# Quad 0 of the first MLP product as seven half-size products, with its sums taken between the first products of two quads

## The chip, the cores and the metric

The kernel runs on one core of a Trainium2 chip. The metric is the device time of one execution in microseconds (us). Engines are named as in the profile: PE is TensorE (PEld its weight loads), DVE is VectorE, ACT is ScalarE, POOL is GpSimd and SP is SyncE, which only issues DMAs here. POOL issues the DMAs that add to what stands in their destination.

## The reference, cut to what matters

S is 512 rows, D is 1024, the inner width of the MLP is 4096, all in fp32.

```python
def reference(x, positions, g_mix, w_in, ..., w_out, g_mlp, w_ff1, w_ff2, g_final):
    h = x
    for l in range(DEPTH):                                   # DEPTH = 1
        n = rmsnorm(h, g_mix[l])
        proj = n @ w_in[l]
        (gq, gk, gv, gr, z_gf, z_gb, cq, ckv, kr, z_ma, z_mb) = jnp.split(proj, SPLIT_IDX, axis=-1)
        y_gla = gla_branch(gq, gk, gv, gr, z_gf, z_gb, ...)
        y_mla = mla_branch(cq, ckv, kr, positions, ...)
        merged = jax.nn.sigmoid(z_ma) * y_gla + jax.nn.sigmoid(z_mb) * y_mla
        h = h + merged @ w_out[l]
        m = rmsnorm(h, g_mlp[l])
        h = h + jnp.square(jax.nn.relu(m @ w_ff1[l])) @ w_ff2[l]
    return rmsnorm(h, g_final)
```

The change is in `m @ w_ff1`, and in what stands around it.

## The kernel before

**Products.** A factor is split into a high part, a rounded copy made by ACT, and a low part, the rest, made by DVE (`split`). A product is then three matmuls: high by high, high by low, low by high (`mm3`). The large products go by a scheme of seven half-size products: both factors are cut into 2 x 2 blocks, and sums and differences of blocks are multiplied, so that seven products (m = 1 to 7) do what eight would. The prices are sums on DVE and in accumulating DMAs, and splits of these sums.

**The MLP.** The normalized rows (`ms0` to `ms3`, 128 rows each) are transposed by PE (`Flipped`, here `fm`) and split into `m00`, `m10` (columns of the first 256 rows) and `m01`, `m11` (those of the last 256). A *quad* is four blocks of 128 of the 4096 features, a 2 x 2 block product with w_ff1: seven products of 24 matmuls of 128x128 by 128x256. There are eight quads. A *group* is a 2 x 2 block product with w_ff2 over two quads' squared features, into banks `ab` and `mb`. Left operands of the groups are `gh`/`gl`; `four` are split sums of the normalized rows; `hl0h`/`hl0l` to `hl3h`/`hl3l` are a ring of four split weight tiles. The four tiles `ms0` to `ms3` later serve as homes of weight blocks and sums (`wide`, `al_`, `ae_`).

**Quad 0 before.** Its four blocks of features (`f00` to `f03`) are computed plainly, each as 48 matmuls of 256 columns: `hidden_run` for the first half of the rows while the last two row tiles are still being normalized, the rest later (`Plain`, `second_halves`, `pair_plain`). The sums of m for the other quads are made by DVE in `summing` after all of m is transposed and split; they are first used by quad 1's product 5.

**Order.** Everything from the attention on is recorded, and a list scheduler (`Due.order`) lays it down: for each engine it takes what is ready, the one with the earliest latest start first, by its own costs (`Work.cost`), and prints each engine's queue in that order. All recorded instructions have line 232 in the profile. Each engine works through its queue in order. Plain loads stand on SP's queue, accumulating loads (`load_add`) on POOL's.

**Elsewhere.** In the attention, queries `q00`, `q01` and so on are gathered by DMAs on SP's queue, one from `ro0` and one from `ro1` (the two halves of the rotated part) each; `kbuf1` to `kbuf3` get a copy of the rotated key in the same way. `s` is the bank of the scores, `top` its row maximum, `uq` the bank of the projected queries.

Of the kernel before, what the change touches and what calls it, by code (L numbers as in the profile page):

```python
# [11 lines left out]
F32 = mybir.dt.float32  # L12
# [129 lines left out]
class Work:  # L142
# [250 lines left out]
def tile_block(ctx: ExitStack, tc: tile.TileContext, t, out: bass.AP):  # L393
# [143 lines left out]
    class Flipped:  # L537
        def __init__(self, gains, name):
            self.gains, self.name = gains, name
            self.out = {  # L540
                (j, c): [u4(f"{name}{j}{c}{x}", F32R, (P, KD // 2, 256)) for x in range(2)]
                for j in range(2) for c in range(2)
            }
            self.banks = {}
# [10 lines left out]

        def evacuate(self, half, ks=range(KD)):
            for k in ks:
                hi, lo = self.out[k // 4, half]
                src = self.banks[half][k % 4][:, (k // 4) * 256 : (k // 4) * 256 + 256]
                split_scaled(hi[:, k % 4, :], lo[:, k % 4, :], src, self.gains[:, k : k + 1])  # L560
# [1148 lines left out]
    ms_rows = {}  # L1709

    def first_half_square(i, c):
        hparts[i] = sm(f"hp{i}", 4)
        ms_rows[i] = u4(f"ms{i}", F32, (P, D))
        square_half(hrow[i], c, hparts[i], ms_rows[i], True)
# [12 lines left out]

    def hidden_run(begun, half, ks=range(KD)):
        wh, wl, acc = begun
        c = slice(half * HT, (half + 1) * HT)  # L1730
        for k in ks:
            hi, lo = fm.out[k // 4, half]
            mm3(acc[:, c], wh[:, k, :], wl[:, k, :], hi[:, k % 4, :], lo[:, k % 4, :], k == 0, k == KD - 1)
        return acc

    def begin_hidden(j):

        early.append(proj_begin(w1, j * P, f"f0{j}"))
# [91 lines left out]
    w1_sums = [u4(f"w1s{x}", F32, (P, D)) for x in range(2)]  # L1830
    fm = Flipped(gvec[:, V_MLP : V_MLP + 8], "m")
    wo_right[7] = [split_part(B12, 0, "bo7")]
    for rb in range(2):
        add_rows(rb, 1, xs_[rb], ALU.subtract)
    wo_right[7].append(split_part(B12, 1, "bo7"))
    for rb in range(2):
        wo_product(3, (rb,))
        add_rows(rb, 1, zs_[rb])
        second_half_square(rb, 1)
        scaled(rb, row_rstd(hparts[rb]))  # L1840
    wo_right[4] = [split_part(B21, 0, "bo4")]
    wo_product(7, (0,))
    add_rows(2, 1, xs_[0], ALU.subtract)
    wo_right[4].append(split_part(B21, 1, "bo4"))
    flipped(0)
    early = [proj_begin(w1, 0, "f00", "mm")]
    first_half_square(2, 1)
    wo_product(7, (1,), range(2))
    flipped(1)
    wo_product(7, (1,), range(2, NP))  # L1850
    add_rows(3, 1, xs_[1], ALU.subtract)
    fm.evacuate(0)
    first_half_square(3, 1)
    begun_f, lows = begin_late(P, "f01", "mm", w1)
    early.append(begun_f)
    for x in w1_sums:
        nc.sync.dma_start(x.rearrange("p (k w) -> p k w", w=HT), w1_block(1, 1, 0))
    wo_product(4, (0,))
    add_rows(2, 0, xs_[0])
    second_half_square(2, 0)  # L1860
    wo_product(4, (1,))
    add_rows(3, 0, xs_[1])
    rs2 = row_rstd(hparts[2])
    second_half_square(3, 0)
    lows()
    rs3 = row_rstd(hparts[3])
    scaled(2, rs2)
    scaled(3, rs3)
    hidden_run(early[0], 0)
    hidden_run(early[1], 0, range(5))  # L1870
    flipped(2)
    flipped(3)
    for x, other in zip(w1_sums, ((1, 1), (0, 0))):
        nc.gpsimd.dma_start(x.rearrange("p (k w) -> p k w", w=HT), w1_block(1, *other), accum_op=ALU.add)
    for j in (2, 3):
        begin_hidden(j)
    fm.evacuate(1)
    hidden_run(early[1], 0, range(5, KD))
# [36 lines left out]
    rows_ = Ring("row", [u2(f"row{n}") for n in range(4)])  # L1915
    sums_ = Ring("sum", [(u2(f"sy{n}"), u2(f"sz{n}")) for n in range(2)])
    parts_ = [[(u2(f"gh{p}{x}", F32R), u2(f"gl{p}{x}", F32R)) for x in range(2)] for p in range(NP)]
    fours = [u4(f"four{n}", F32R, (P, KD // 2, HT)) for n in range(12)] + fm.out[0, 1]
# [33 lines left out]
    def summing():  # L1952
        homes = {(0, 0): (al_[0], ("al", 0)), (1, 1): (al_[1], ("al", 1)),
                 (0, 1): (wide[2], ("ae", 0)), (1, 0): (wide[3], ("ae", 1))}
        r = {}
        for c in range(2):
            for j in range(2):
                hi, lo = fm.out[j, c]
                x, key = homes[j, c]
                x = flat(x, KD // 2)  # L1960
                r[j, c] = x, key
                dve(FULL, (lambda x=x, hi=hi, lo=lo: nc.vector.tensor_tensor(x, raw(hi), raw(lo), op=ALU.add)),
                    m_key_of(j, c), (key,))

        def combine(o, a, b, op):
            dve(FULL, lambda: nc.vector.tensor_tensor(r[o][0], r[a][0], r[b][0], op=op),
                (r[a][1], r[b][1]), (r[o][1],))

        A, B, C, Dd = (0, 0), (1, 1), (0, 1), (1, 0)
        combine(A, A, C, ALU.subtract)  # L1970
        combine(C, B, C, ALU.subtract)
        combine(B, B, A, ALU.add)
        combine(Dd, B, Dd, ALU.subtract)
        return {5: r[A], 6: r[B], 7: r[C], 4: r[Dd]}

    def m_key_of(j, c):
        n = 2 * j + c
        return (("m", 2 * n), ("m", 2 * n + 1))

    def split_m(m, src, n):  # L1980
        x, key = src
        hi, lo = m_tiles[2 * n], m_tiles[2 * n + 1]
        k = (("ms", 2 * n), ("ms", 2 * n + 1))
        keys = (key,)
        if m == 6:
            act(FULL, lambda: nc.scalar.activation(hi, x, AF.Copy, scale=-1.0), keys, k[:1])
            dve(FULL, lambda: nc.vector.scalar_tensor_tensor(
                lo, x, -1.0, raw(hi), op0=ALU.mult, op1=ALU.subtract), keys + k[:1], k[1:])
        else:
            act(FULL, lambda: nc.scalar.activation(hi, x, AF.Copy), keys, k[:1])  # L1990
            dve(FULL, lambda: nc.vector.tensor_tensor(lo, x, raw(hi), op=ALU.subtract), keys + k[:1], k[1:])
        m_of[m], m_key[m] = (hi, lo), k

    m_of[1], m_of[2], m_of[3] = fm.out[0, 0], fm.out[1, 0], fm.out[1, 1]
    m_key[1], m_key[2], m_key[3] = m_key_of(0, 0), m_key_of(1, 0), m_key_of(1, 1)
# [56 lines left out]
    class Plain:  # L2052


        def __init__(self, j):
            self.j, self.key = j, ("f", j)

        def multiply(self):
            j = self.j
            used = sum((m_key_of(a, b) for a in range(2) for b in range(2)), (("hl", j, 0), ("hl", j, 1)))  # L2060

            def run():
                for half in range(2):
                    hidden_run(early[j], half)

            plan.add("PE", 5.5, run, used, (self.key,))

        def evacuate(self, dst, key):
            act(HALFT, lambda: nc.scalar.activation(dst, early[self.j][2], AF.Relu), (self.key,), (key,))

    class Quad:


        def __init__(self, q):
            self.q, self.banks, self.row = q, {}, {}
# [4 lines left out]
        def fetch(self):  # L2080
            (a, e), (ka, ke) = ae_[self.q % 2], ae_key[self.q % 2]
            self.a, self.e, self.ka, self.ke = flat(a, KD // 2), flat(e, KD // 2), ka, ke
            if self.q == 1:
# [6 lines left out]
        def weights(self, m):  # L2090
            k = KD // 2
            if m in (1, 2, 4):
                item, x, key = staged(self.rows(*{1: (0, 0), 2: (0, 1), 4: (1, 1)}[m]), k)
                ready = prepare(x, key, k)
                if m == 2:
                    self.c = item, x, key
                else:
                    wfs.back(item)
# [41 lines left out]
        def evacuate(self, m, bkey, acc):  # L2140
# [13 lines left out]
            if m == 2:  # L2154
                lefts[p].first(x, key)
            elif m == 3:
                self.pair(p, "px", "qx")
# [200 lines left out]
    plains = [Plain(j) for j in range(4)]  # L2358

    def pair_plain(p):  # L2360
        (kp, px), (kq, qx) = rows_.take(), rows_.take()
        item = sums_.take()
        ykey, (y, z) = item
        for x, (dst, key) in enumerate(((y, ykey), (z, ykey + ("z",)))):
            plains[2 * p + x].evacuate(dst, key)
            c = slice(x * HT, (x + 1) * HT)
            act(QUART, (lambda dst=dst, c=c: nc.scalar.activation(px[:, c], dst[:, 0:HT], AF.Square)), (key,), (kp,))
            act(QUART, (lambda dst=dst, c=c: nc.scalar.activation(qx[:, c], dst[:, HT:S], AF.Square)), (key,), (kq,))
        sums_.free.insert(0, item)
        lefts[p].first(px, kp)  # L2370
        lefts[p].summed(px, qx, kp, kq)
        rows_.back((kp, px))
        rows_.back((kq, qx))

    def second_halves():
        for k in range(KD):
            for e in early[:2]:
                hidden_run(e, 1, (k,))

# [84 lines left out]
```

## Time and profile before

| | |
|---|---|
| Median of 3 runs | 742.14 us (741.44 to 743.15) |
| The profiled execution | 742.11 us, of which the span of the trace is 740.4 us |
| PE | 730.2 us busy (99%), 4238 matmuls and transposes |
| DVE | 606.2 us (82%) |
| ACT | 512.2 us (69%) |
| POOL | 193.6 us (26%) |
| Granted TensorE clock | 1.00 in all stages shown |

A busy share is an average over stages. PE counts as busy while a matmul is in its pipeline. Of the span, the stretch from 404 to 480 us holds the end of the output projection, the transposes of the normalized rows, quad 0, quad 1 and the first group; from 480 us on, groups and quads alternate at an even pace.

### The profile page before, as it was taken

Reading aid. Unit: us, or ns where it says so; the run is one execution under the profiler, and the core shown is the slowest. Engines: PE = TensorE matmul, PEld = TensorE weight load, DVE = VectorE, ACT = ScalarE, POOL = GpSimd, SP = SyncE. Lnnn points to the kernel's source line nnn. Section 1 sums busy time; section 2 is a strip of 40 time slices with the busy share of each in tenths; the row PEclk is TensorE's granted clock in tenths of the full one; section 3 lists DMA queues with packets and bytes.
Section 4 is the critical chain, followed back from the end, with each engine's and each line's share of the span. In section 5 each row is a group of like instructions: output and inputs, shape, how many; then the busy total and the mean of one; then the engine's idle time right before and its main releaser. Section 6 shows DMA issues by size and latency. Waiting matters only on the chain.

```text
span 740.4 us, 11575 instructions
## 1 busy us (share of the span) xinstructions
PE 730.2 (99%) x4238; PEld 643.3 (87%) x4238; DVE 606.2 (82%) x956; ACT 512.2 (69%) x855; POOL 193.6 (26%) x203
## 2 busy tenths in 40 slices
PE   9999999999999999999999999999999999999996
PEld 7888888888888888899988999889988998889985
DVE  7695776759999679998988899868896798778885
ACT  7574665669999566989856788546864587448754
POOL 1133040301211115038753102321122202312433
PEclk9999999999999999999999999999999999999998
DMA  9969895752313214239976449999899997988993
GB/s 312 327 142 168 224 192 107 118 112 57 98 46 68 39 38 109 56 99 246 270 207 98 115 119 222 208 228 201 207 203 212 212 206 178 220 220 191 194 167 115
DMA packets 103930, 121.24 MB, mean 164 GB/s; under 512 B 16080, under 2 KB 67296, under 8 KB 103872
## 3 DMA queue, kind: packets, MB, share of 16 engines
q0 software_dynamic: 30384, 48.52, 38.9%
q1 hardware_dynamic: 73200, 71.45, 31.7%
q8 instruction: 33, 0.54, 0.3%
q10 hardware_dynamic: 288, 0.52, 0.2%
q14 instruction: 25, 0.20, 0.1%
HBM read 116.81 MB, written 2.10 MB: 161 GB/s over the span
## 4 chain that ended last, share of the span: by engine, by line
PE 87%; DVE 5%; DMA 3%; ACT 2%; issue 1%; POOL 1%; POOLq 0%; DVEq 0%; ACTq 0%
PE mb L232 21%; PE ab L232 14%; PE zb L232 4%; PE f L232 3%; PE av L232 3%; PE wox L232 3%; PE gvx L232 3%; PE zax L232 3%; PE grx L232 3%; PE first L232 3%; PE s L232 2%; DMA ms<-in_w_ff 2%; PE cq L232 2%; PE tp L232 2%; PE gvz L232 1%; PE ckv L232 1%
## 5 line engine op out<-in xcount | busy, mean ns | idle before, releaser
L232 POOL DMA_DIRECT2D ms<-in_w_ff x37 | 46.7, 1370 | 115.7 <-DVE hl0l L232 34.7
L232 POOL DMA_DIRECT2D w1s<-in_w_ff x18 | 23.0, 1276 | 90.7 <-DVE hl0l L232 26.9
L232 DVE TENSOR_TENSOR h<-h,ab 128x512 f32<-128x512 f32 x48 | 31.7, 682 | 6.4 <-PE ab L232 6.4
L232 ACT ACTIVATE row<-row 128x512 f32<-128x512 f32 x49 | 30.7, 626 | 1.0
L232 PE MATMUL s<-kbuf,q 96*128 96x512 f32 x96 | 28.3, 408 | 1.4 <-DMA q<-ro 1.4
L232 PE MATMUL av<-pT,v 128*128 128x256 f32 x192 | 28.0, 289 | 0.0
L232 PEld LDWEIGHTS av<-pT,v 128*128 128x128 f32 x192 | 24.8, 190 | 0.5
L232 DVE TENSOR_REDUCE top<-s 128x1 f32<-128x512 f32 x32 | 21.7, 686 | 4.2 <-PE s L232 3.9
L232 ACT ACTIVATE e<-s,top 128x512 f32<-128x512 f32 x32 | 22.0, 695 | 3.9 <-DVE top L232 3.7
L232 PE MATMUL mb<-four,hl0h 128*128 128x256 f32 x128 | 23.4, 283 | 0.0
L232 DVE TENSOR_TENSOR hl1l<-ms,hl1h 128x1024 fp32r<-128x1024 f32 x12 | 14.7, 1224 | 9.9 <-ACT hl1h L232 9.8
L232 DVE TENSOR_TENSOR pT<-tp,pT 128x512 fp32r<-128x512 f32 x32 | 21.6, 682 | 1.1 <-PE av L232 0.5
L232 ACT ACTIVATE row<-mb 128x512 f32<-128x512 f32 x28 | 16.4, 584 | 7.0 <-PE mb L232 7.0
L232 ACT ACTIVATE hl3h<-ms 128x1024 fp32r<-128x1024 f32 x13 | 13.8, 1058 | 10.5 <-PE ab L232 4.6
L232 ACT ACTIVATE pT<-tp 128x512 fp32r<-128x512 f32 x32 | 19.3, 602 | 2.4 <-PE tp L232 2.3
L232 PEld LDWEIGHTS mb<-four,hl0h 128*128 128x128 f32 x128 | 20.1, 192 | 0.5 <-ACT hl2h L232 0.2
L232 PE MATMUL mb<-four,hl3h 128*128 128x256 f32 x112 | 20.4, 283 | 0.0
L232 PE MATMUL mb<-m,hl2h 128*128 128x256 f32 x112 | 20.4, 283 | 0.0
L232 PE MATMUL mb<-four,hl2h 128*128 128x256 f32 x112 | 20.4, 283 | 0.0
L232 ACT ACTIVATE hl1h<-ms 128x1024 fp32r<-128x1024 f32 x12 | 12.7, 1057 | 10.7 <-DMA ms<-in_w_ff 3.7
L232 DVE TENSOR_TENSOR hl3l<-ms,hl3h 128x1024 fp32r<-128x1024 f32 x13 | 15.9, 1223 | 4.9 <-ACT hl3h L232 4.7
L232 PE MATMUL tp<-ident,e 128*128 128x128 f32 x128 | 19.3, 273 | 0.1
(1142 smaller groups left out, 2808.4 us busy)
## 6 DMA issues: line engine op xcount, KB each, us to landing
ms<-in_w_ff POOLq DMA_DIRECT2D x37, 512.0 KB, 7.7
w1s<-in_w_ff POOLq DMA_DIRECT2D x18, 512.0 KB, 6.8
ms<-in_w_ff SPq DMA_DIRECT2D x16, 512.0 KB, 5.1
w1s<-in_w_ff SPq DMA_DIRECT2D x15, 512.0 KB, 6.1
w<-in_w_out POOLq DMA_DIRECT2D x10, 512.0 KB, 9.1
wf0f<-in_w_ff SPq DMA_DIRECT2D x10, 512.0 KB, 6.6
wf1f<-in_w_ff SPq DMA_DIRECT2D x10, 512.0 KB, 6.2
wf2f<-in_w_ff SPq DMA_DIRECT2D x10, 512.0 KB, 5.9
```

The lines of the kernel that those rows point to most:

```text
L232: return call(*map(real, work.args), **{k: real(v) for k, v in work.named.items()})
```

## The change

1. The scheduler's cost of a DMA on SP's queue was 0.06; it is now 0.62 where the DMA reads on-chip memory and 0.45 where it reads HBM. This reorders queues wherever such DMAs stand.
2. Quad 0 becomes a `Quad` like the others. It has two sum tiles of its own (`w0_sums`), and quad 1 keeps its two (`w1_sums`). Products 1 and 2 of quads 0 and 1, which take `m00` and `m10` as they are, stand first; the sums of m (`r00`, `r10`, `r01`, `r11`, `msum`) are taken between and after them, from banks that ACT evacuates whole (`whole`); the split sums for product 5 and 6 are made in halves. Then come products 5 and 6 of both quads in turn, and then 7, 7, 3, 4, 3.
3. In quads 0 and 1 the weights of product 6 get their last block by an accumulating DMA on POOL's queue, not by a DVE add of a staged tile.
4. `m01` is no longer split, there are two more `four` tiles, and quad 1's product 7 leaves the first group.

PE's program falls from 4183 matmuls to 4159, and POOL issues five more DMAs, SP one more.

```diff
     def cost(self):
         n = self.n
         if self.is_dma:
-            return 1.27 if self.engine == "gpsimd" else 0.06
+            return 1.27 if self.engine == "gpsimd" else 0.62 if self.ins else 0.45
...
+        def whole(self, half, ks, to):
+            for k in ks:
+                nc.scalar.activation(to[:, k % 4, :], self.bank(half, k), AF.Copy, scale=self.gains[:, k : k + 1])
...
-    hidden_run(early[0], 0)
-    hidden_run(early[1], 0, range(5))
-    flipped(2)
-    flipped(3)
...
+    def joined(to, j, cols=slice(0, KD // 2)):
+        hi, lo = fm.out[j, 0]
+        nc.vector.tensor_tensor(to[:, cols], raw(hi[:, cols]), raw(lo[:, cols]), op=ALU.add)
+
+    def combine(o, a, b, op, cols=slice(0, KD // 2)):
+        nc.vector.tensor_tensor(o[:, cols], a[:, cols], b[:, cols], op=op)
...
+            elif m == 6 and self.q < 2:
+                load_add(a, self.rows(0, 1), self.ka)
             elif m == 6:
                 item, c, key = self.c
                 dve(FULL, lambda: nc.vector.tensor_tensor(a, a, c, op=ALU.add), (self.ka, key), (self.ka,))
...
-    plan.add("PE", 5.5, second_halves, tuple(("hl", j, x) for j in range(2) for x in range(2)), (("f", 0), ("f", 1)))
-    plains[2].multiply()
-    pair_plain(0)
-    sources = summing()
-    for n, m in enumerate((5, 6, 7, 4)):
-        split_m(m, sources[m], n)
-    plains[3].multiply()
-    quads = {q: Quad(q) for q in range(1, 2 * NQ)}
...
+    quads[0].multiply(1)
+    quads[1].ready(1)
+    quads[0].multiply(2)
+    flipped(2)
+    flipped(3)
+    for x, other in zip(w1_sums, ((1, 1), (0, 0))):
+        nc.gpsimd.dma_start(x.rearrange("p (k w) -> p k w", w=HT), w1_block(1, *other), accum_op=ALU.add)
+    quads[1].ready(2)
+    joined(r00, 0)
+    joined(r10, 1)
+    quads[1].multiply(1)
+    fm.whole(1, range(4), r01)
+    for cols in (slice(0, 2), slice(2, 4)):
+        combine(r00, r00, r01, ALU.subtract, cols)
+        split_m(5, r00, 0, cols)
+    for k in (0, 2):
+        cols = slice(k, k + 2)
+        fm.whole(1, range(4 + k, 6 + k), r11)
+        combine(msum, r11, r00, ALU.add, cols)
+        split_m(6, msum, 1, cols)
+    combine(r01, r11, r01, ALU.subtract)
+    combine(r10, msum, r10, ALU.subtract)
+    quads[1].multiply(2)
+    split_m(7, r01, 2)
+    fm.evacuate(1, range(4, KD))
+    split_m(4, r10, 3)
     groups = [Group(qd) for qd in range(NQ)]
-    w = quads[1]
-    w.multiply(5)
-    pair_plain(1)
-    for m in (1, 2, 6, 3):
-        w.multiply(m)
+    for m in (5, 6):
+        for q in range(2):
+            quads[q].multiply(m)
+    for q, m in ((0, 7), (1, 7), (0, 3), (0, 4), (1, 3)):
+        quads[q].multiply(m)
+    del rows_.free[3:]
     for qd, g in enumerate(groups):
         odd = quads[2 * qd + 1]
         g.multiply(1, 0)
-        odd.multiply(7)
+        if qd:
+            odd.multiply(7)
```

**SP's queue in the attention.** These are the DMAs on SP where the queries of the first heads are gathered; first before, then after.

```order
L232 DMA kbuf1_538_2867<-kbuf0_537_2747 32x1024
L232 DMA kbuf2_539_2918<-kbuf0_537_2747 32x1024
L232 DMA kbuf3_540_2920<-kbuf0_537_2747 32x1024
L232 DMA q00_565_2833<-ro0_555_2895 16x1024
L232 DMA q01_566_2843<-ro0_555_2895 16x1024
L232 DMA q10_587_2930<-ro0_555_2895 16x1024
L232 DMA q11_588_2934<-ro0_555_2895 16x1024
L232 DMA q00_565_2833<-ro1_558_2905 16x1024
```

```order
L232 DMA kbuf1_538_2867<-kbuf0_537_2747 32x1024
L232 DMA q00_565_2833<-ro0_555_2895 16x1024
L232 DMA q00_565_2833<-ro1_558_2905 16x1024
L232 DMA q01_566_2843<-ro0_555_2895 16x1024
L232 DMA q01_566_2843<-ro1_558_2905 16x1024
L232 DMA kbuf2_539_2951<-kbuf0_537_2747 32x1024
```

The second half of `q00` moves from the eighth place of these rows to the third, and the other copies of the key go behind the queries.

**DVE's queue in the first group.** Tile `ms1` holds a block of w_ff2 that is split and then gets another block added by a DMA from POOL; the last row of each piece is the low half of that split. The `sy`, `sz` and `row` tiles hold squared features of the groups' left operands. First before, from the split of `ms0` on; then after, the last nine of the 17 rows that stand between the same split of `ms0` and that of `ms1`, and the latter.

```order
L232 TENSOR_TENSOR hl1l_955_4709<-ms0_894_4290,hl1h_954_4683 128x1024
L232 TENSOR_TENSOR w1s0_903_4189<-w1s0_903_4189,wf1f_950_4501 128x1024
L232 TENSOR_TENSOR sz1_975_4785<-row3_971_4754,sy1_974_4716 128x256
L232 TENSOR_TENSOR hl2l_957_4724<-w1s1_904_4296,hl2h_956_4704 128x1024
L232 TENSOR_TENSOR hl0l_953_4678<-w1s0_903_4189,hl0h_952_4654 128x1024
L232 TENSOR_TENSOR row1_969_4722<-mb2_962_4863,row1_969_4722 128x512
L232 TENSOR_TENSOR hl3l_959_4874<-ms1_896_4316,hl3h_958_4850 128x1024
```

```order
L232 TENSOR_TENSOR sz0_941_4932<-row0_934_4522,sy0_940_4925 128x256
L232 TENSOR_TENSOR hl3l_925_4551<-wf2f_917_4333,hl3h_924_4510 128x1024
L232 TENSOR_TENSOR gl00_945_4965<-sy0_940_4925,gh00_944_4945 128x512
L232 TENSOR_TENSOR row5_939_4792<-mb3_929_4593,row5_939_4792 128x512
L232 TENSOR_TENSOR sy1_942_4873<-sy1_942_4873,row0_934_4522 128x256
L232 TENSOR_TENSOR sz1_943_4982<-row0_934_4522,row2_936_4742 128x256
L232 TENSOR_TENSOR hl0l_919_4409<-wf0f_915_3480,hl0h_918_4395 128x1024
L232 TENSOR_TENSOR four9_969_4984<-row0_934_4522,four9_969_4984 128x512
L232 TENSOR_TENSOR sz1_943_4982<-row0_934_4522,sy1_942_4873 128x256
L232 TENSOR_TENSOR hl2l_923_4529<-ms1_869_4291,hl2h_922_4501 128x1024
```

Before, five rows stand between the two splits; after, 17 (ten of 256 columns, four of 512, three of 1024).

**POOL's queue there.** The rows with `in_w_ff` are accumulating loads; those onto `ms0` and `ms1` bring blocks of w_ff2, those onto `ms2` and `ms3` and the `w0s`, `w1s` tiles blocks of w_ff1. First before, then after.

```order
L232 DMA w1s0_903_4189<-in_w_ff1 128x4x256
L232 DMA ms0_894_4290<-in_w_ff2 128x2x512
L232 DMA ms2_930_4386<-in_w_ff1 128x4x256
L232 DMA ms3_932_4459<-in_w_ff1 128x4x256
L232 DMA ms1_896_4316<-in_w_ff2 128x2x512
```

```order
L232 DMA w1s0_907_4205<-in_w_ff1 128x4x256
L232 DMA w0s0_905_4161<-in_w_ff1 128x4x256
L232 DMA w1s0_907_4205<-in_w_ff1 128x4x256
L232 DMA ms3_871_4465<-in_w_ff1 128x4x256
L232 DMA ms2_870_4453<-in_w_ff1 128x4x256
L232 DMA ms0_868_4252<-in_w_ff2 128x2x512
L232 DMA ms1_869_4291<-in_w_ff2 128x2x512
```

The add onto `ms1` stays last of these; the three others onto `ms` tiles stand in another order before it, behind the new adds onto `w0s0` and `w1s0`.

More of the change, by code (lines that the diff above doesn't have):

```diff
@@ L1829, in tile_block @@
     wo_product(6)
-    w1_sums = [u4(f"w1s{x}", F32, (P, D)) for x in range(2)]
+    w0_sums, w1_sums = ([u4(f"w{q}s{x}", F32, (P, D)) for x in range(2)] for q in range(2))
     fm = Flipped(gvec[:, V_MLP : V_MLP + 8], "m")
[L1832 to L1868, printed above, removed]
-    hidden_run(early[0], 0)
-    hidden_run(early[1], 0, range(5))
-    flipped(2)
-    flipped(3)
[L1873 to L1878, printed above, removed]
     class Plan:
@@ L2050, in split, with ready @@
             dve(HALFT, lambda: nc.vector.tensor_tensor(l, src, raw(h), op=ALU.subtract), (key, k[0]), k[1:])
[L2052 to L2069, printed above, removed]
     class Quad:
         def __init__(self, q):
-            self.q, self.banks, self.row = q, {}, {}
+            self.q, self.banks, self.row, self.begun = q, {}, {}, {}
+        def ready(self, m):
+            self.begun[m] = self.weights(m)
         def rows(self, i, j):
@@ L2356, in tile_block @@
     lefts = [Left(p) for p in range(NP)]
[L2358 to L2373, printed above, removed]
```

125 lines of the change are left out of this document (65 added, 60 removed).

## The prediction

> **What bounds the kernel now.** I read the page first, then the busy times by stage, then the chain and the list of waits for PE, and last the rows around each wait.
>
> ```profile
> span 740.4 us, 11575 instructions
> PE 730.2 (99%) x4238; PEld 643.3 (87%) x4238; DVE 606.2 (82%) x956; ACT 512.2 (69%) x855; POOL 193.6 (26%) x203
> PE 87%; DVE 5%; DMA 3%; ACT 2%; issue 1%; POOL 1%; POOLq 0%; DVEq 0%; ACTq 0%
> ...
> core 0: us, PE busy (x) PEld busy (x) DVE busy (x) ACT busy (x) POOL busy (x), PEclk, DMA share, GB/s
> 404.00:422.00 18.00, 18.00 (x123) 16.43 (x122) 13.32 (x25) 12.14 (x25) 4.17 (x5) 1.00 0.55 140
> 422.00:440.00 18.00, 18.00 (x152) 17.95 (x151) 17.97 (x24) 13.83 (x26) 1.31 (x1) 1.00 0.33 77
> 440.00:466.00 26.00, 26.00 (x190) 24.55 (x189) 25.76 (x39) 22.71 (x36) 5.38 (x5) 1.00 0.91 220
> 466.00:471.00 5.00, 5.00 (x24) 4.14 (x23) 1.31 (x4) 1.34 (x3) 0.81 (x1) 1.00 1.11 301
> 471.00:480.00 9.00, 8.65 (x50) 7.29 (x48) 9.00 (x12) 6.42 (x8) 3.75 (x4) 1.00 0.91 147
> 480.00:721.00 241.00, 240.98 (x1524) 219.25 (x1524) 194.91 (x257) 150.93 (x204) 58.26 (x50) 1.00 0.93 204
> ```
>
> PE is busy 730.2 of 740.4 us, and in the stretch that the change rewrites (404 to 480 us) all but 0.35 of 76 us; from 480 to 721 us it misses 0.02. So PE's own instructions set the time, and an edit counts in two ways only: by matmuls that go, or by a wait of PE that goes or comes. The second engine is DVE: in 404 to 480 us it works 13.32 + 17.97 + 25.76 + 1.31 + 9.00 = 67.36 us, which leaves it 8.6. The granted clock is 1.00 in each of these stages, so I let no term scale.
>
> The profiled execution took 742.11 us, 1.7 more than its span and 0.03 below the median of 742.14. So differences in the span carry over to the median as they are. About 0.2%, 1.5 us, is what a measurement of this kernel can tell from no change.
>
> **Part 1: PE's matmuls, -2.9 us.** Quad 0 was four blocks of 48 matmuls, 192; as seven products of 24 it is 168. All are 128x128 by 128x256.
>
> ```profile
> 554.78 2.87 PE mb L232 x24
> ```
>
> This is one product of the steady part, 24 such matmuls back to back in 2.87 us, 120 ns each. 24 fewer are 2.87 us, and all of it lies on the path as long as PE waits for nothing new. The Trainium skill ("TensorE: Matmul & The Clock Gate", section "Back-to-back issue gap") gives N/2.4 + 2.5 ns for a matmul by itself, which for 256 columns makes 109 ns and, by an estimate, 2.6 us here and a time 0.3 us longer than mine; the trace's 120 ns decides.
>
> **Part 2: the scheduler's price of an SP DMA, -1.4 us.** It moves the queries' copies in the attention.
>
> ```profile
> PE s L232 <- DMA q<-ro: 1.4, 1, 1.4
> ...
> 288.43 1.29 DVE L232 TENSOR_TENSOR ro<-roa,ro 128x512 fp32r<-128x512 f32 x2
> 288.48 1.87 SPq L232 DMA_DIRECT2D kbuf<-kbuf  x3
> 290.45 6.25 SPq L232 DMA_DIRECT2D q<-ro  x10
> 292.47 0.62 PE L232 MATMUL uq<-cqhl,wq1h 128*128 128x512 f32 x2
> 295.36 2.32 PE L232 MATMUL s<-kbuf,q 96*128 96x512 f32 x9 [1.36 <-DMA q<-ro]
> 296.33 2.08 DVE L232 TENSOR_REDUCE top<-s 128x1 f32<-128x512 f32 x3 [1.50 <-PE s L232]
> ...
> 292.98 2.25 DMA q<-ro
> ```
>
> The first scores waited 1.36 us for `q00`'s second half. That DMA is the fifth of ten that SP issued from 290.45 on, 0.625 us each, so it was issued at 290.45 + 4 x 0.625 = 292.95 (the chain has 292.98) and landed 2.25 later. Its source had been there since 288.43 + 1.29 = 289.72. In the new order only one copy of the key and `q00`'s first half stand ahead of it: it is issued at 290.4 or before and lands at 292.0 to 292.6. The scores now follow two `uq` matmuls, not six: PE comes there at about 292.9. So the wait goes: 1.4 us (none if something else is late there, 1.4 if not). What is late next is the row maximum, which had idled 1.50 us for the scores and starts earlier with them. The two copies of the key that are put back serve later heads.
>
> **Part 3: the wait at the first group's second half, -0.5 us.**
>
> ```profile
> 477.91 0.28 PE L232 MATMUL mb<-four,hl3l 128*128 128x256 f32 x1
> 478.54 0.47 PE L232 MATMUL ab<-hl2h,gh 128*128 128x512 f32 x1 [0.35 <-DVE h L232]
> 453.16 16.63 DMA ms<-in_w_ff
> 469.87 1.07 ACT hl1h L232
> 470.96 1.23 DVE L232 TENSOR_TENSOR hl1l<-ms,hl1h 128x1024 fp32r<-128x1024 f32 x1 [3.69 <-ACT hl1h L232]
> ```
>
> The gap is 0.35 us by PE's idle time, 0.63 from start to start. Behind it stands DVE's burst at 471 to 480 (9.00 us busy of 9), and that burst began late because its split waited 3.69 us for the weights in `ms1`, whose accumulating DMA took 16.63 us. In the new order that split is queued with other work around it. I take 0.5 us for the wait's going, 0 if the DMA is as late again.
>
> **Part 4: what the new order adds for DVE, ACT and the queues, +1.0 us (0.3 to 3).** DVE's prices are pitches of neighbouring rows:
>
> ```profile
> 430.93 1.22 DVE L232 TENSOR_TENSOR hl0l<-w1s,hl0h 128x1024 fp32r<-128x1024 f32 x1
> 432.06 1.22 DVE L232 TENSOR_TENSOR four<-ms,four 128x1024 fp32r<-128x1024 f32 x1
> 460.88 0.42 DVE L232 TENSOR_TENSOR sy<-sy,row 128x256 f32<-128x256 f32 x1
> 461.21 0.42 DVE L232 TENSOR_TENSOR sy<-row 128x256 f32<-128x256 f32 x1
> 461.55 0.69 DVE L232 TENSOR_TENSOR gl<-sz,gh 128x512 fp32r<-128x512 f32 x1
> 462.15 0.68 DVE L232 TENSOR_TENSOR gl<-sy,gh 128x512 fp32r<-128x512 f32 x1
> 410.15 2.44 DVE L232 SCALAR_TENSOR_TENSOR m<-mb,gvec,m 128x256 fp32r<-128x256 f32 x6
> ```
>
> 1.13 us for 1024 columns, 0.60 for 512, 0.33 for 256, 0.40 for the scaled split of `m`. From the scaling of the second row tile to the last `gl`, the queue before holds 30, 18 and 20 of the three sizes and 16 scaled splits; after, 27, 26, 20 and 12. The three fewer of 1024 and four fewer splits are 3.4 + 1.6 = 5.0 us, the eight more of 512 4.8: no change. So DVE keeps its 8.6 us of idle time there, less the 2.9 by which PE is faster, and is not the bound over the stretch. ACT has 76 - (12.14 + 13.83 + 22.71 + 1.34 + 6.42) = 19.6 us idle there and takes on about three weight splits and some squares; that is hidden.
>
> What isn't hidden is order in the small. Quads 0 and 1 alternate product by product, and product 7 is added onto the bank of product 6, which ACT copies away first: one product, 2.87 us, lies between. The nearest rows for such a wait are the 0.35 us above and one ACT copy of a bank:
>
> ```profile
> 451.13 0.58 ACT L232 ACTIVATE row<-mb 128x512 f32<-128x512 f32 x1
> ```
>
> One copy and one such gap are 0.93, and I take 1.0 in all. The upper bound is one product, 2.87: a wait that lets PE stand for as long as the product that was to cover it. The lower bound is one gap, 0.35. A gain isn't in it, since PE waits for nothing in the rows before.
>
> **Part 5: the DMA onto `ms1`, 0 us (0 to 6).** This is the term with the widest bounds.
>
> ```profile
> 446.17 1.22 DVE L232 TENSOR_TENSOR hl1l<-ms,hl1h 128x1024 fp32r<-128x1024 f32 x1
> 451.64 1.22 DVE L232 TENSOR_TENSOR hl3l<-ms,hl3h 128x1024 fp32r<-128x1024 f32 x1
> 472.43 0.39 PE L232 MATMUL ab<-hl1h,gh 128*128 128x512 f32 x1
> 447.69 3.81 POOL L232 DMA_DIRECT2D ms<-in_w_ff  x3 [13.80 <-DVE hl1l L232]
> 453.16 1.18 POOL L232 DMA_DIRECT2D ms<-in_w_ff  x1 [1.66 <-DVE hl3l L232]
> ...
> w1s<-in_w_ff POOLq DMA_DIRECT2D x1, 512.0 KB, 6.2
> ms<-in_w_ff POOLq DMA_DIRECT2D x9, 512.0 KB, 8.5
> ```
>
> The add may start only when the old content has been split. Before, that split began 5.5 us after the split of `ms0` (446.17 to 451.64). In the new order 17 rows stand between: with the split itself ten of 0.33, four of 0.60 and four of 1.13, 10.2 us. So the add is issued about 4.7 us later, at 457.9 and, with ACT's half not ahead of time, up to 458.8. Before, PE used the new content's high half at 472.43. In the new order PE has 2.6 us less of work ahead of that use (24 fewer matmuls, one other moved ahead of it), so it comes there at 469.8, and with the 1.0 of part 4 at 470.8; the low half is used 1.8 us later, other matmuls standing between. ACT's split takes 1.07 us, so the add has to land by 468.7 to 469.7, which is 9.9 to 11.8 us after its issue. The rows give 6.2 us for an add nearly alone, 8.5 for the median of nine from 430 to 500 us, and 16.6 for this very one. I take 8.5 and so no wait: the 16.6 came right behind three adds issued in 3.81 us at 447.69, and in the new order two of these three, onto `ms3` and `ms2`, stand ahead of the one onto `ms0` and should go earlier.
>
> **The sum.** -2.87 - 1.4 - 0.5 + 1.0 = -3.8, and 742.1 - 3.8 = 738.3 us. Its own range is 736.3 to 740.3. The upper end has the new waits at 3. The lower has the three gains whole and the new waits at 0.35, 737.6, and 1.3 less for what the new SP price may take away elsewhere: outside of 404 to 721 us PE is idle for 740.4 - 730.2 - 0.4 = 9.8 us, and I let at most an eighth of that go.
>
> **The rivals.** *The adds and loads share the DMA engines evenly.* While SP's loads keep a queue full, an add takes twice the 6.2 us of the one nearly alone, 12.4. Issued at 458.8 it lands at 471.2, the split ends at 472.3, and PE waits 1.5 us from 470.8 on: 739.8. For it: the DMA share is 0.91 in 440 to 466 us. Against: the median of 8.5 is under the same load. The Trainium skill ("DMA: Bandwidth & Descriptors", section "Queues, rings and completion order") states that each DMA engine goes round among its queues by packets; by that rule two full queues would halve each other, and the trace neither shows nor excludes it. 0.11.
>
> *The scores are held by something else.* Then part 2 is worth nothing: 738.3 + 1.4 = 739.7. For it: the attention's rows on DVE are dense around 296 us. Against: DVE's idle 1.50 us ends with the scores, not before. 0.09.
>
> *The alternating products wait.* The sums for products 5 and 6 are taken while product 1 and 2 of quad 1 run; if the halves arrive late, PE stands for one more product, 2.9 us: 738.3 + 2.9 = 741.2, no difference that can be measured. For it: DVE is full (17.97 of 18) in 422 to 440 us, the place of these sums. Against: they are spread over 404 to 440 us, and DVE has 4.7 us idle in 404 to 422. 0.13.
>
> *Slower: the add onto `ms1` takes its 16.6 us again.* Issued at 458.8 it lands at 475.4, the split ends at 476.5, 5.7 us after PE comes there at 470.8, and the wait of part 3 doesn't go: 738.3 + 5.7 + 0.5 = 744.5. It costs time from 10.9 us after issue on, and makes the kernel slower by over 0.2% from 10.9 + 4.8 = 15.7 us on, since 738.3 + 0.5 + 4.8 is 743.6. For it: the row of before itself, and the DMA share of 1.11 in 466 to 471 us, the transfers being all there is to wait for. Against: half of the nine adds of 430 to 500 us took 8.5 us or less. 0.16.
>
> That the change doesn't do what it says can't be: the orders of PE hold 24 fewer matmuls.
>
> **How the numbers follow.** The forecast has 0.51; with the first two rivals, faster by over 0.2% (below 740.6) has 0.71, with a little of the forecast's upper end at the bound. Within 0.2% has the third, 0.13, and slower the last, 0.16. The time is that of the likeliest case, 738.3. The range takes in the forecast, the first three rivals and their spread, 736.3 to 742.5, and leaves out the slower one.
>
> **What would show it.** Right: the list of waits for PE has no `s` on the DMA `q` over 0.3 us; PE's count falls by 24; the row of the add onto `ms1` lands within 11 us, and no wait of `ab` or `mb` in the first group is over 1 us; waits in the new stretch from 404 us to the start of the first group sum to about 1 us. Wrong: a wait of several microseconds on a split whose chain starts with `ms<-in_w_ff`, or waits of PE on the splits for products 5 and 6 that sum to over 3 us, or DVE busy without a gap from 404 to 480 us with PE waiting for it.

## The result, and the profile after

| | before | after |
|---|---|---|
| Median | 741.79 us (741.44 to 743.15, 6 runs) | 737.83 us (737.25 to 738.97, 6 runs) |
| Profiled execution | 742.11 us | 737.60 us |

The ratio is 0.9946, 95% interval 0.9933 to 0.9958: 4.0 us less, where 3.8 had been forecast. The two profiled executions, from which the parts below are read, are 4.5 us apart. A later set of five runs of the changed kernel gave 737.84 us.

The page of after, its parts 1 and 4:

```profile
span 735.9 us, 11540 instructions
PE 726.7 (99%) x4214; PEld 640.5 (87%) x4214; DVE 606.2 (82%) x959; ACT 516.7 (70%) x863; POOL 201.6 (27%) x208
PE 93%; DVE 3%; ACT 2%; issue 1%; DMA 1%; POOL 1%; POOLq 0%; DVEq 0%; ACTq 0%
```

PE has 24 matmuls fewer and DVE's busy time is what it was, to a tenth. In the chain that ended last PE's share went from 87 to 93%: two detours over DMAs and DVE are gone from it.

The busy times by stage, after, in the columns of before (PE, PEld, DVE, ACT, POOL, clock, DMA share, GB/s):

```profile
404.00:422.00 18.00, 18.00 (x126) 16.68 (x125) 15.63 (x24) 13.77 (x26) 8.77 (x7) 1.00 0.84 161
422.00:440.00 18.00, 17.35 (x143) 16.94 (x142) 16.13 (x22) 17.26 (x32) 4.62 (x4) 1.00 0.90 215
440.00:466.00 26.00, 26.00 (x175) 23.87 (x174) 25.93 (x43) 22.71 (x37) 4.08 (x4) 1.00 1.02 227
466.00:471.00 5.00, 5.00 (x30) 4.40 (x29) 5.00 (x7) 3.92 (x5) 2.64 (x3) 1.00 0.78 124
471.00:480.00 9.00, 9.00 (x46) 7.62 (x46) 6.97 (x10) 2.72 (x3) 3.44 (x3) 1.00 1.14 195
```

PE loses 0.65 us between 422 and 440 us, where it lost none, and none from 471 to 480 us, where it lost 0.35. The list of waits for PE names the new places, and no longer has `s` on `q` or `ab` on `h`:

```profile
PE mb L232 <- ACT row L232: 0.5, 1, 0.5
PE mb L232 <- DVE four L232: 0.2, 1, 0.2
```

To see all that PE loses, small pauses too, I took each matmul's distance to the next start, less the median distance for matmuls of its bank and shape in the same trace, and summed this by stretch. This is called lost time below:

| lost time of PE, us | whole | 285 to 320 us | 404 to 460 us | 460 to 480 us |
|---|---|---|---|---|
| before | 6.12 | 2.20 | 0.3 | 0.79 |
| after | 4.49 | 0.03 | 1.3 | 0.09 |

So the span's 4.5 us are 2.87 for the matmuls and 1.63 for lost time: -2.17 in the attention, -0.70 at the first group, +1.0 in the new stretch, and +0.2 elsewhere, most of it in the kernel's first 10 us, where the waits for the first loads differ from run to run (1.1 to 1.8 us of lost time in the kernels shown here).

The attention, rows of after's timeline, and the two windows before and after (before first):

```profile
288.75 0.58 SPq L232 DMA_DIRECT2D kbuf<-kbuf  x1
289.42 2.46 SPq L232 DMA_DIRECT2D q<-ro  x4
293.20 2.23 PE L232 MATMUL s<-kbuf,q 96*128 96x512 f32 x9
```

```profile
285.00:300.00 15.00, 13.64 (x77) 11.71 (x77) 12.91 (x25) 9.06 (x26) 4.22 (x6) 1.00 0.66 160
300.00:320.00 20.00, 19.86 (x130) 17.32 (x130) 18.41 (x33) 19.58 (x42) 2.41 (x4) 1.00 0.07 14
```

```profile
285.00:300.00 15.00, 15.00 (x91) 13.26 (x90) 13.92 (x27) 10.77 (x29) 4.48 (x7) 1.00 0.62 137
300.00:320.00 20.00, 20.00 (x136) 17.91 (x135) 19.32 (x36) 19.76 (x43) 3.26 (x4) 1.00 0.18 52
```

The queries are issued behind one copy of the key, and the scores start at 293.20 without a wait, 2.16 us earlier than before. PE has no gap left in these 35 us; before it had 1.5.

The add onto `ms1`, rows of POOL, of the DMAs (kind, count, KB, us to landing), of ACT and of PE in after:

```profile
457.31 1.18 POOL L232 DMA_DIRECT2D ms<-in_w_ff  x1 [9.40 <-DMA ms<-in_w_ff]
ms<-in_w_ff POOLq DMA_DIRECT2D x1, 512.0 KB, 5.9
467.81 1.05 ACT L232 ACTIVATE hl0h<-ms 128x1024 fp32r<-128x1024 f32 x1
469.04 0.63 PE L232 MATMUL ab<-hl0h,gh 128*128 128x512 f32 x2
```

It was issued at 457.3, a little ahead of the predicted 457.9 to 458.8, and landed 5.9 us later, not 16.6 as before. ACT took its content up at 467.81, having been busy with other splits: 4.6 us of slack.

### The profile page after: what moved, and what is told of

It reads as the page before. It is cut to its first block, busy times and chain, and to the rows that moved or that the text cites. A ratio compares the mean times of both kernels' runs of the same rounds, so it can differ in the third digit from the quotient of the medians.

```text
span 735.9 us, 11540 instructions
## 1 busy us (share of the span) xinstructions
PE 726.7 (99%) x4214; PEld 640.5 (87%) x4214; DVE 606.2 (82%) x959; ACT 516.7 (70%) x863; POOL 201.6 (27%) x208
## 4 chain that ended last, share of the span: by engine, by line
PE 93%; DVE 3%; ACT 2%; issue 1%; DMA 1%; POOL 1%; POOLq 0%; DVEq 0%; ACTq 0%
PE mb L232 25%; PE ab L232 16%; PE zb L232 4%; PE av L232 3%; PE s L232 3%; PE wox L232 3%; PE gvx L232 3%; PE zax L232 3%; PE grx L232 3%; PE first L232 3%; PE cq L232 2%; PE tp L232 2%; PE uv L232 2%; PE gvz L232 2%; PE ckv L232 1%; PE gq L232 1%
## 5 line engine op out<-in xcount | busy, mean ns | idle before, releaser
L232 ACT ACTIVATE row<-row 128x512 f32<-128x512 f32 x56 | 35.1, 627 | 1.1 <-DVE row L232 0.3
L232 PE MATMUL mb<-four,hl3h 128*128 128x256 f32 x144 | 26.6, 283 | 0.0
L232 ACT ACTIVATE row<-mb 128x512 f32<-128x512 f32 x32 | 18.7, 586 | 7.8 <-PE mb L232 7.6
L232 PE MATMUL mb<-four,hl1h 128*128 128x256 f32 x128 | 23.5, 283 | 0.0
L232 PEld LDWEIGHTS mb<-four,hl3h 128*128 128x128 f32 x144 | 22.8, 191 | 0.5
L232 ACT ACTIVATE hl2h<-ms 128x1024 fp32r<-128x1024 f32 x13 | 13.8, 1059 | 11.9 <-PE ab L232 6.1
L232 ACT ACTIVATE hl0h<-ms 128x1024 fp32r<-128x1024 f32 x11 | 11.6, 1058 | 12.9 <-PE ab L232 8.7
L232 PE MATMUL mb<-m,hl1h 128*128 128x256 f32 x112 | 20.6, 283 | 0.0
L232 PEld LDWEIGHTS mb<-four,hl1h 128*128 128x128 f32 x128 | 20.2, 192 | 0.2
L232 PE MATMUL mb<-four,hl3l 128*128 128x256 f32 x72 | 20.3, 283 | 0.0
```

The source lines that it names most:

```text
L232: return call(*map(real, work.args), **{k: real(v) for k, v in work.named.items()})
```

## The experiments

All times are medians, beside runs of the kernel before on the same chip (741.8 to 742.4 us).

| kernel | us | ratio to before | PE's lost time: whole; 285 to 320; 404 to 460; 460 to 480 |
|---|---|---|---|
| price alone | 739.26 | 0.9961 (0.9948 to 0.9975) | 3.23; 0.08; 0.2; 0.02 |
| old price | 739.53 | 0.9967 (0.9954 to 0.9979) | 6.49; 2.22; 1.0; 0.13 |
| product 5 twice | 739.12 | 0.9956 (0.9944 to 0.9969) | 3.25; 0.03; 0.1; 0.06 |
| product 3 before 7 | 738.00 | 0.9949 (0.9936 to 0.9961) | 5.10; 0.08; 1.3; 0.11 |
| copies shared | 738.48 | 0.9956 (0.9943 to 0.9968) | 4.98; 0.05; 1.7; 0.04 |
| add by DVE | 738.30 | 0.9952 (0.9938 to 0.9965) | 5.08; 0.03; 2.0; 0.07 |
| quad by quad | 737.53 | 0.9939 (0.9924 to 0.9955) | 4.90; 0.04; 1.0; 0.02 |
| quad by quad, again | 737.42 | 0.9938 (0.9926 to 0.9951) | 4.28; 0.05; 1.0; 0.02 |
| changed, again | 737.84 | 0.9941 (0.9928 to 0.9955) | 4.78; 0.03; 1.3; 0.07 |
| load and add | 739.12 | 0.9965 (0.9952 to 0.9979) | 5.95; 0.06; 1.4; 0.89 |
| add in 8 parts | 737.68 | 0.9943 (0.9929 to 0.9956) | 4.49; 0.03; 1.3; 0.05 |
| add in 16 parts | 744.97 | 1.0041 (1.0027 to 1.0055) | 11.88; 0.02; 1.3; 7.58 |

### The two halves of the change apart

Before, with the price alone:

```diff
-            return 1.27 if self.engine == "gpsimd" else 0.06
+            return 1.27 if self.engine == "gpsimd" else 0.62 if self.ins else 0.45
```

> The kernel before with the new scheduler's prices of SP's DMAs alone; quad 0 stays plain. Theory (the price takes away the waits in the attention and nothing else): PE's lost time between 285 and 320 us was 2.2 us before and is 0.03 in the changed kernel, so 741.8 - 2.2 = 739.6 us, and the list of waits for PE has no s on the DMA q. By the prediction's own term of 1.4 it would be 740.4. Rival (the new order moves everything and gains or loses elsewhere as much): 741.8 or more, with new waits of PE behind 400 us.

The changed kernel with that line undone:

> The changed kernel with the old price of 0.06 for SP's DMAs; quad 0 as seven products stays. Theory (two separate gains that add up): 737.8 + 2.2 = 740.0 us, with the wait of s on the DMA q back at 1.4 us, and PE's lost time between 404 and 480 us as in the changed kernel, about 1 us. Rival (the seven products are only worth it with the new order): 741.8 or more, with waits of PE of over 2 us between 404 and 480 us.

Each half alone brings about 3 us (742.37 to 739.26 and to 739.53), both together 4.0. The price alone brought 3.1 where the theory had 2.2, since it takes away the wait at the first group as well as those in the attention; the seven products alone brought 2.8 where theirs had 1.8. So the second theory, two separate gains that add up, fell: the group's wait goes in either kernel and is counted once when both are there. By lost time: the price alone -2.12 in the attention and -0.77 at the group; the seven products alone -2.87 for matmuls, -0.66 at the group, +0.7 in the new stretch; both together -2.87 - 2.17 - 0.70 + 1.0. The halves overlap by 1.0 us in this account (0.7 at the group, 0.3 in the new stretch); by the ratios to before, which sum to 0.72% where both together bring 0.54%, it is 1.3.

What the two halves have in common at the group is seen at the add onto `ms1`. With the price alone, POOL, the DMA and ACT:

```profile
451.06 1.18 POOL L232 DMA_DIRECT2D ms<-in_w_ff  x1 [3.95 <-DVE hl3l L232]
ms<-in_w_ff POOLq DMA_DIRECT2D x1, 512.0 KB, 9.7
463.99 1.05 ACT L232 ACTIVATE hl1h<-ms 128x1024 fp32r<-128x1024 f32 x1
```

It lands at 460.8, and ACT's split at 464.0 doesn't wait; before it had waited 3.65 us and DVE's burst had begun late. With the old price and the seven products the add is issued at 458.9 and lands 6.6 us later. In all three new orders fewer adds are issued just ahead of it than the three in 3.81 us of before. What stands beside it differs too: while the add was under way, the DMA share was 1.13 before, 1.09 with the price alone, 0.78 with the seven products alone and 0.79 with both, for 16.6, 9.7, 6.6 and 5.9 us. So a late add goes with the wait and an early one with none in all four kernels; which of the things queued ahead or beside made it late before isn't separated.

With the old price the wait in the attention is back, and the new one stays (waits for PE):

```profile
PE s L232 <- DMA q<-ro: 1.4, 1, 1.4
PE mb L232 <- ACT row L232: 0.5, 1, 0.5
```

### Does PE set the time in the new stretch?

```diff
+            for _ in range(2 if (self.q, m) == (0, 5) else 1):
-            plan.add("PE", 2.88, run, keys + m_key[m], (bkey,))
+                plan.add("PE", 2.88, run, keys + m_key[m], (bkey,))
```

> The changed kernel with product 5 of quad 0 computed twice, the second time over the first, so 24 matmuls of 256 columns more and nothing else. Theory (PE's matmuls set the time in that stretch): 2.87 us more, less up to 0.6 where ACT and DVE use the time to catch up: 740.1 to 740.7 us. Rival (DVE or ACT, 16 to 26 us busy of 18 and 26 there, set the time and PE only follows): 737.8 to 738.5 us, PE's lost time falling by what was added.

739.12 us, 1.3 more than the changed kernel (0.7 by the ratios to before): between what the two expected, so both missed. The windows of this kernel, and DVE's first sum in it:

```profile
404.00:422.00 18.00, 18.00 (x127) 16.71 (x126) 16.34 (x25) 15.64 (x30) 6.33 (x7) 1.00 0.89 188
422.00:440.00 18.00, 18.00 (x152) 18.00 (x152) 17.10 (x23) 16.47 (x30) 3.97 (x4) 1.00 0.82 166
440.00:466.00 26.00, 26.00 (x182) 24.28 (x181) 23.32 (x36) 22.31 (x36) 4.72 (x4) 1.00 1.02 241
...
422.44 1.42 DVE L232 TENSOR_TENSOR ms<-ms,ms 128x512 f32<-128x512 f32 x2 [0.34 <-ACT ms L232]
```

PE has no gap left, and its lost time from 404 to 460 us fell from 1.3 to 0.1. So of the added 2.87 us, 1.2 came back as waits that went, and the rest, 1.7, is on the path (the two sets of runs leave 0.4 of that unaccounted). PE sets the time there, but not with room to spare. I had allowed 0.6 for this. That the waits went isn't all due to the longer work: the scheduler laid this kernel anew, the transposes of the last rows start 0.9 us earlier (420.82, in the changed kernel 421.71) and the first sum 1.0 earlier (422.44, there 423.43), so the wait at product 5, 0.36 us, was gone before the repeated product began. The other, 0.61 ahead of product 7, stands behind it.

### What is late in the new stretch

Four edits tried to find which link it is. Product 3 of quad 0 ahead of product 7:

```diff
-    for q, m in ((0, 7), (1, 7), (0, 3), (0, 4), (1, 3)):
+    for q, m in ((0, 3), (0, 7), (1, 7), (0, 4), (1, 3)):
```

> The changed kernel with quad 0's product 3 ahead of its product 7, so that two products instead of one lie between product 6 and the product that is added onto its bank. Theory (product 7 waits only for ACT's copy of that bank): the wait of 0.45 us of mb on ACT's row goes and the time is 0.5 us less, 737.3. Rival (ACT, 17.3 us busy of 18 from 422 to 440 us, is late with whatever comes next): the wait moves to another product or grows, 737.8 to 739 us.

The wait ahead of product 7 went, and the one at product 5's first use of `four` grew from 0.36 to 1.13 us of lost time: 738.0. The rival held: its time and its place for the wait. The scheduler lays the whole stretch anew after such an edit, and ACT's and DVE's work falls in another order.

Half of the whole evacuations on DVE:

```diff
             for k in ks:
-                nc.scalar.activation(to[:, k % 4, :], self.bank(half, k), AF.Copy, scale=self.gains[:, k : k + 1])
+                if k % 2:
+                    nc.vector.tensor_scalar(to[:, k % 4, :], self.bank(half, k), self.gains[:, k : k + 1], None, op0=ALU.mult)
+                else:
+                    nc.scalar.activation(to[:, k % 4, :], self.bank(half, k), AF.Copy, scale=self.gains[:, k : k + 1])
```

> The changed kernel with half of the whole evacuations of the last row tiles (the odd blocks) on DVE instead of ACT. Theory (PE's 1.0 us in 422 to 440 us is a lateness of the chain from the transposes over ACT's four copies of 0.39 us, during which DVE idles 2.38 us, and of nothing else): the chain is 0.8 us shorter, at least 0.8 of the 1.0 us go, 736.9 to 737.2 us. Rival (DVE or ACT are full there, and work that is moved comes back as a wait at the next split): 737.6 us or more, with the waits of PE there still at 0.8 us or more.

DVE's rows around it, of the changed kernel and then of this one, with PE's wait as its last row:

```profile
423.43 1.42 DVE L232 TENSOR_TENSOR ms<-ms,ms 128x512 f32<-128x512 f32 x2 [2.38 <-ACT ms L232]
```

```profile
422.66 1.27 DVE L232 TENSOR_SCALAR ms<-mb,gvec 128x256 f32<-128x256 f32 x3 [1.52 <-PE mb L232]
423.84 1.28 DVE L232 TENSOR_TENSOR ms<-ms,ms 128x512 f32<-128x512 f32 x2
426.39 0.39 PE L232 MATMUL mb<-four,hl0h 128*128 128x256 f32 x1 [0.76 <-DVE four L232]
```

A miss: 738.48, in the rival's range. The first sum starts no earlier: ahead of it now stand seven of the eight copies, three on DVE and four on ACT, where these two sums need four, so the chain wasn't shortened, and PE's wait there rose from 0.20 to 0.76. It doesn't show that a shorter chain would be worth nothing; in the kernel with product 5 twice the first sum came 1.0 us earlier and the wait at product 5 was gone.

Products 5 and 6 quad by quad:

```diff
-    for m in (5, 6):
-        for q in range(2):
+    for q in range(2):
+        for m in (5, 6):
             quads[q].multiply(m)
```

> The changed kernel with products 5 and 6 of quad 0 and then those of quad 1, not in turn. Theory (the alternation gives the sums for product 6 one more product, 2.87 us, to be ready, and these sums are what is late): product 6 of quad 0 waits for its split, 1 to 2.9 us more, 738.8 to 740.7. Rival (only ACT's copy ahead of product 7 is late; it now has more time): 737.3 us.

> The kernel with products 5 and 6 quad by quad once more, in five rounds beside the changed kernel on the same chip. Theory (it takes away PE's 0.6 us ahead of product 7 and adds nothing): 0.3 to 0.6 us below the changed kernel. Rival (what it gains there comes back in small stalls): the same.

> The changed kernel itself once more, on the chip of the next one. Theory and rivals: 737.8 us.

The theory fell: product 6 doesn't wait for its sums with only product 5 ahead of it, and neither wait of the changed kernel is left in the list for PE. What is left, 1.0 us of lost time from 404 to 460 us against 1.3, are pauses of about 0.1. It is the fastest kernel of the study, 737.42 beside 737.84 on the same chip, but the two intervals overlap (0.9926 to 0.9951 and 0.9928 to 0.9955): that it is faster isn't shown.

The last block of product 6's weights by a DVE add of a staged tile, as in the other quads:

```diff
-                if m == 2 and self.q > 1:
+                if m == 2:
                     self.c = item, x, key
...
-            elif m == 6 and self.q < 2:
-                load_add(a, self.rows(0, 1), self.ka)
             elif m == 6:
```

> The changed kernel with the last block of product 6's weights of quads 0 and 1 added by DVE from a staged tile, as the other quads do, so two accumulating DMAs fewer and two DVE adds of 1.13 us more. Theory (DVE is 15.6, 16.1 and 25.9 us busy of 18, 18 and 26 there and PE's wait is a lateness on it and ACT): 0.5 to 2.3 us more, 738.3 to 740.1. Rival (the adds fit into DVE's gaps, or the DMAs had been the late ones): 737.8 or less.

738.30 us, 0.5 more, the low end of what the theory expected. The waits moved to the weights of the next products:

```profile
431.88 0.50 PE L232 MATMUL mb<-four,hl3h 128*128 128x256 f32 x2 [0.45 <-ACT hl3h L232]
433.06 0.39 PE L232 MATMUL mb<-four,hl2l 128*128 128x256 f32 x1 [0.68 <-DVE hl2l L232]
```

Two DVE adds of 1.13 us cost 0.7 us of lost time (2.0 against 1.3), so the move of these adds to POOL's queue is worth about 0.5 to 0.7 us of the change. Which single link of ACT and DVE sets the remaining 1 us stays open: it moves with each edit, and only the kernel with the repeated product has none of it.

### The slower rival: what if the add onto `ms1` is late?

A first try put a plain load ahead of the add:

```diff
+            if m == 1 and (self.qd, g) == (0, 1):
+                self.load(B11, g, B12)
+                self.onto(B11, B11, g)
-            if m == 1:
+            elif m == 1:
                 self.onto(B11, B12, g)
```

> The changed kernel with the sum in ms1 for the first group formed by a plain load of the second block and an accumulating load of the first over it, so that one SP load of 512 KB stands ahead of the add. Theory (the add has slack: issued at 457.3 it lands at 463.2, and PE's use at 469.04 less ACT's 1.07 leaves 4.7 us; what is beyond is a wait of PE one for one): the add is issued 5 to 7 us later, lands at about 469 to 470 and PE waits 0.5 to 2.5 us, 738.3 to 740.3 us. Rival (the transfer is hidden by far more, or the scheduler finds other work for PE): 737.8 us.

The time, 739.12, is in the theory's range, but not for its reason, so this says nothing on it: the scheduler knew of the load and moved the tile's first load and split ahead, the add was issued at 455.8, earlier than in the changed kernel, and the lost time came elsewhere (0.78 us at 427, and 0.63 at 472 behind a split on DVE, not behind a DMA).

The next two leave the order of all engines as it is and only cut this one DMA into parts when it is laid down:

```diff
+        if getattr(work, "parts", False):
+            dst, src = map(real, work.args)
+            for k in range(2):
+                for w in range(0, S, P):
+                    done = call(dst[:, k, w : w + P], src[:, k, w : w + P], **work.named)
+            return done
...
-                self.onto(B11, B12, g)
+                self.onto(B11, B12, g).parts = (self.qd, g) == (0, 1)
```

> The changed kernel, its order untouched, with the add onto ms1 in the first group issued as eight DMAs of 64 KB instead of one of 512 KB, so that POOL issues for about 8 x 1.2 us and the last part lands later. Theory (the add has slack up to ACT's split at 467.8 us and costs PE one for one beyond it): the last part is issued at about 466 and lands at 470 to 472, 13 to 15 us after the first issue, and PE waits 2 to 4 us in ab: 740 to 742 us. Rival (such a delay is taken up by other work, PE and the engines having slack): 737.8 to 738.5 us.

POOL worked through the eight faster than I thought, in 7.04 us, and the last landed at 467.20, 2.9 us after POOL was done with it: just ahead of ACT's split at 467.82. The time didn't move, 737.68. The theory's price wasn't tested; the 4.6 us of slack were, and they are real. With sixteen (`P // 2` in place of `P`):

> The changed kernel, its order untouched, with the add onto ms1 in the first group issued as sixteen DMAs of 32 KB. In eight parts they were issued 0.88 us apart and the last landed 3.8 us after its issue, at about 467.2, still ahead of ACT's split at 467.8, and the time stayed. Theory (beyond that slack the add costs PE one for one, as the slower rival of the prediction has it): the last part is issued at 457.3 + 15 x 0.88 = 470.5, lands at about 474.3, 17 us after the first issue, and PE, which uses the split at 469.0, waits about 6 us in ab: 743 to 744.5 us. Rival (other work takes the place, or later slack gives it back): 738 to 740 us.

744.97 us, 7.1 more, and slower than before, by 0.27 to 0.55%. That is above the theory's 743 to 744.5, although PE's wait was shorter than the 6 us in it. POOL, the chain, ACT, PE:

```profile
457.12 14.07 POOL L236 DMA_DIRECT2D ms<-in_w_ff  x16 [9.33 <-DVE hl2l L238]
467.11 5.62 DMA ms<-in_w_ff
472.90 1.06 ACT L238 ACTIVATE hl0h<-ms 128x1024 fp32r<-128x1024 f32 x1 [5.12 <-DMA ms<-in_w_ff]
474.01 1.22 PE L238 MATMUL ab<-hl0h,gh 128*128 128x512 f32 x2 [4.94 <-ACT hl0h L238]
```

The last part landed at 472.73, 15.6 us after the first issue. ACT waited 5.12 us for it and PE 4.94: one for one, beyond the slack. But the kernel lost 7.1. The windows of this kernel around the wait (the clock is the third number from the end):

```profile
466.00:469.00 3.00, 3.00 (x15) 2.40 (x13) 3.00 (x5) 1.78 (x3) 3.00 (x8) 1.00 0.45 39
469.00:474.00 5.00, 0.07 (x1) 0.00 (x0) 0.32 (x2) 1.10 (x2) 5.00 (x6) 0.83 0.48 48
474.00:476.00 2.00, 1.99 (x7) 1.80 (x8) 2.00 (x2) 0.91 (x1) 1.43 (x2) 0.50 1.02 185
476.00:478.00 2.00, 2.00 (x10) 1.90 (x10) 0.95 (x2) 0.00 (x0) 1.74 (x2) 0.50 1.15 174
478.00:480.00 2.00, 2.00 (x8) 1.58 (x7) 0.45 (x1) 0.00 (x0) 0.14 (x1) 0.71 1.22 205
480.00:484.00 4.00, 4.00 (x24) 3.51 (x23) 3.77 (x6) 1.66 (x2) 0.00 (x0) 1.00 1.13 206
```

The granted clock fell to 0.50 at 472.32, during the wait, and stayed there to 479.14, 5.1 us after PE had begun again, so that some 2.5 us of matmuls took twice as long. Of the 7.6 us of lost time from 460 to 480 us, 5.1 are the wait, by the distance of starts, and 2.4 the slow matmuls behind it.

The Trainium skill ("TensorE: Matmul & The Clock Gate", section "What's actually happening") states that the clock is halved after an idle window of about 3.4 us and released after as long a busy one, and that these windows run on freely, whatever the kernel does. The trace agrees on the half and on that a wait of 4.94 us is enough. The 6.83 us at half clock fit, by an estimate from the page's 3.4, two such windows, of which the first, to about 475.7, still holds the end of the wait; one such wait doesn't show that this is the reason.

No wait of PE in the kernels before and after is over 1.4 us.

## Why the prediction was right

**The sum.** By lost time the four parts came to -2.87 - 2.17 - 0.70 + 1.0 = -4.7, 0.9 more than the forecast's -3.8. The medians moved by 4.0, between the two. So the mechanism and the signs held, two sizes were short, and that the time came within 0.5 us of 738.3 is in part luck.

**Part 1, 24 matmuls, -2.87.** Right, with the reservation that its neighbour shows: the trace has 24 fewer, and with 24 put back the time rose by 1.3, since the waits of part 4 weren't there in that kernel. So the 2.87 and the 1.0 aren't independent; together they are the 1.9 that the seven products bring net of the waits that come with them.

**Part 2, the queries, -1.4.** Right in mechanism and place, short in size: -2.17 of lost time. The wait that was named was 1.53 by distance of starts; 0.57 more had been lost in 300 to 320 us, 0.31 of it at one transpose that followed the late scores, and that went with it. I had priced the one wait with a name and not those behind it.

**Part 3, the first group's wait, -0.5.** Right in sign, 0.70 in size. The reason was only argued then, the late add onto `ms1`. The runs of the two halves fit it: each lands the add early enough, and has no such wait. But each reorders other work there too, so the add alone isn't shown to be the cause. That either half would do this I had not seen, and with it that the halves' gains don't add.

**Part 4, new waits, +1.0.** 1.0 measured, and one of its two places is the named one, product 7 behind ACT's copy of product 6 (0.61 of lost time); the other, 0.36, is at the first `four` of product 5. That the sizes agree so well is luck: they were estimated from one copy and one gap.

**Part 5, the add, 0.** Right. It took 5.9 us, below the median of 8.5 that I took and near the 6.2 of one nearly alone; that it would be so short I hadn't worked out. The bound by which it had to land, 468.7 to 469.7, was ACT's split ahead of PE's use; in fact ACT took it up at 467.8 and PE used it at 469.04, so it had 4.6 us to spare.

**The rivals.** Even sharing of the DMA engines (12.4 us for the add) wasn't put to the test: its condition, loads that keep SP's queue full, didn't arise. From the add's issue to its landing the DMA share was 0.79, and SP's queue moved 0.39 MB beside the add's 0.52. So this run neither bears out nor refutes the rule that the prediction cites from the Trainium skill ("DMA: Bandwidth & Descriptors", section "Queues, rings and completion order"). Scores held by something else: no, they started 2.2 us earlier. Products waiting for their sums: 0.36 us of lost time at product 5, where this rival had 2.9; product 6 didn't wait even without the alternation. The slower rival has the right mechanism, as the sixteen parts show, but too low a price: a wait of 5.7 us would have cost the clock too. With the 2.4 us that this cost in the sixteen parts, 744.5 would have been about 747, by an estimate.

## What to carry to other kernels

When one engine is busy all the time, count its instructions first, and then ask for each wait what it takes with it: small pauses behind a named wait go too, and a wait that two edits remove is to be counted once. Work taken from the busy engine shortens the cover of everything else, so part of such a gain can come back as waits for copies and sums that are now just late. A scheduler's wrong price for one kind of DMA was worth as much here (3.1 us by itself) as the 24 of the plain quad's 192 matmuls (2.9): look at what the order assumes beside what the trace shows.

## What the runs showed of the hardware that was not expected

A wait of PE of 4.94 us cost about 2.4 us more than itself, since the granted clock was 0.50 during the next 5 us. The add of 512 KB onto `ms1` took 5.9, 6.6, 9.7 and 16.6 us to land in four orders of the same work, at DMA shares of 0.79, 0.78, 1.09 and 1.13. POOL was done with accumulating DMAs of 64 or 32 KB onto one tile 0.88 us apart (7.04 us for eight, 14.07 for sixteen), where one of 512 KB took 1.18: each part more kept POOL for most of a microsecond, whether it held 64 KB or 32.
